# Working out the SSM poles on 128 partitions by 32 columns, from the first FFN steps on

## The chip, the cores and the metric

The kernel runs on one core of a Trainium2 chip. The metric is the device time of one execution in microseconds (us). A profiled execution gives, beside its time, a trace of every engine: TensorE (PE, with its weight loads as PEld), VectorE (DVE), ScalarE (ACT), GpSimd (POOL) and SyncE (SP, which issues most of the transfers). "SPq" is SP's queue of such issues.

## The reference

One layer of a hybrid encoder on 1024 tokens of width 1024, in float32:

```
x = x + 1/2 * SwiGLU_1(RMSNorm(x))              # 1024 -> 2816 -> 1024
[q | k | v | u] = RMSNorm(x) @ W_in
a = windowed attention (+-128 tokens, ALiBi, sinks) on (q, k, v)
s = bidirectional block-diagonal S5 SSM on u, GELU, GLU
x = x + concat(RMSNorm(a), RMSNorm(s)) @ W_out
x = x + 1/2 * SwiGLU_2(RMSNorm(x))
out = RMSNorm(x)
```

The SSM has 2 directions, 32 groups and 64 states to a group: 4096 complex poles. For each,

```
lr = min(lam_re, -1e-4); dt = exp(log_dt)        # one dt per direction and group
mag = exp(lr*dt)
a   = mag * (cos(li*dt) + i sin(li*dt))          # the pole
c   = (a - 1) / (lr + i li)                      # the coefficient
```

and from a and c come powers of the poles, decay tables and small matrices per group that the scan later reads.

## The kernel before

**The FFN.** Each matrix product is done in Strassen-Winograd form (class `Fast`), with seven products p in the order 1, 2, 6, 5, 7, 3, 4, and each float32 product is three matmuls of a high and a low part (`mm3`, L114 to L116). The work is a list of 217 units, one to a step: steps 0 to 139 make gate (i=0) and up (i=1) products, 14 to each of ten pairs s of hidden columns (pair 0 is done apart, in the startup, ahead of step 0); steps 140 to 216 are the down product, seven passes (p = 1, 2, 6, 5, 7, 3, 4) of eleven steps. A step is 12 matmuls of 512 columns.

`Fast.step(n)` issues, in this order: the loads of step n+6 (down product only, `load_down`, L267 and L274), the split of the operands of step n+3 (`prep`: ACT makes the high part, DVE the low part `ll`, with some Winograd sums on DVE), the 12 matmuls of step n, the evacuation of step n (`evac`: ACT or DVE reads the PSUM bank), and what is due at that step (`hidden`, `down_weights`: sums on DVE and stores through POOL). Products 1, 6, 7 and 4 of one (s, i) accumulate in the same PSUM bank, so step n+2 of them waits until the evacuation of step n has read the bank. Every engine works in the order of issue.

**The filler.** `ssm_tables()` is a generator. From step 17 on `fill(n)` runs one piece of it after a step: on 12 of every 14 steps of the gate and up products, then on all steps of the down passes p=1 and p=6 (twice on every second step of p=6). What is left after step 171 is run there. The generator has these pieces:

- step 17: loads of lam_re, lam_im, log_dt (L433 to L435) and of the skip gains;
- steps 18 to 35: the poles, a and c, on tiles of 32 partitions (groups) by 2 x 64 columns, 95 DVE instructions;
- step 40: four PE transposes (L540) into a PSUM bank, four ACT copies out of it;
- steps 41 to 51: powers and decay tables on 128 partitions (`cmul`, `p8r`, `ev`, `ec`, `bd`);
- steps 55 to 171: 32 groups g, three pieces each: `ca` (and `keep`, the stores of an earlier group's `vs` and `ks`), `vt` with a store, and `finish` (PE transposes and matmuls in the one "tp" bank, ACT copies to `vs` and `ks`). After every eight groups `spread` issues eight transfers from k_d to o_d in DRAM (L637): `spread(1)` at step 139, `spread(2)` at step 170, `spread(3)` at the end of step 171.

Pass p=2 of the down product also accumulates in "tp", which is why p=2 has no filler. During the passes p=1, 2, 6 and 5, four steps of each load a piece of x (L960).

**The startup** (ahead of step 0) loads eight row tiles of x, norms them (`prep_x`), turns them by PE transposes (`turn_tok`), forms Winograd sums on DVE (`sums_x`) and turns these (`turn_t`), and does pair 0 (`mm_first`, `evac_first`). Between steps 16 and 17 DVE builds `rel`, a table of distances; its first DVE instruction waits for a POOL iota behind POOL's stores.

Of the kernel before, what the change touches and what calls it, by code (L numbers as in the profile page):

```python
# [9 lines left out]
F32 = mybir.dt.float32  # L10
F32R = mybir.dt.float32r
I32 = mybir.dt.int32
BF16 = mybir.dt.bfloat16
AF = mybir.ActivationFunctionType
ALU = mybir.AluOpType
# [3 lines left out]
P = 128  # L19
# [11 lines left out]
G = 32  # L31
HC = 16
T = 8
# [34 lines left out]
def tile_hymba_block(  # L68
# [8 lines left out]
    V, S, PE, GP = nc.vector, nc.scalar, nc.tensor, nc.gpsimd  # L77
    load = nc.sync.dma_start
# [5 lines left out]
    pools = Pools(tc)  # L84


    def bank(tag, shape=(P, 512)):
        bufs = {"pg": 2, "pu": 2, "pd": 3, "tp": 1}[tag]
        return ps.tile(list(shape), F32, name=tag, tag=tag, bufs=bufs)

    def tt(out, a, b, op, eng=None):
        (eng or V).tensor_tensor(out=out, in0=a, in1=b, op=op)  # L92
# [46 lines left out]
    ident = const.tile([P, P], F32, name="ident")  # L139
# [277 lines left out]
    a64r = const.tile([P, G], F32, name="a64r")  # L417
    a64s = const.tile([P, 2, G], F32, name="a64s")

    def ssm_tables():  # L420
        tab = pools.open("tab")
        ev = tab.tile([P, 3, T, G], F32, name="ev")
        ec = tab.tile([P, 3, 11, G], F32, name="ec")
        dcol = tab.tile([48, G], F32, name="dcol")
        p1 = pools.open("p1")
        n1 = [0]

        def tl(shape=(32, 2, 64), dt=F32):
            n1[0] += 1
            return p1.tile(list(shape), dt, name=f"p1_{n1[0]}", tag=f"p1_{n1[0]}")  # L430

        lr, li, ldt = tl(), tl(), tl((32, 2))
        load(lr, lam_re[0].rearrange("d g p -> g d p"))  # L433
        load(li, lam_im[0].rearrange("d g p -> g d p"))
        load(ldt, log_dt[0].rearrange("d g -> g d"), )  # L435
        load(dcol[32:48], ssm_d[0].rearrange("g h -> h g"))
        yield
        e1, e2, e3 = tl(), tl(), tl()
        dt = tl((32, 2))

        def exp_(y, v, k, f, w):

            ts(v, v, -170.0, ALU.max, 88.8, ALU.min)
            ts(k, v, 1.4426950408889634, ALU.mult, MAGIC, ALU.add)
            ts(k, k, -MAGIC, ALU.add)
            stt(v, k, -0.693359375, v, ALU.mult, ALU.add)
            stt(v, k, 2.12194440e-4, v, ALU.mult, ALU.add)
            yield
            ts(y, v, 1.9875691500e-4, ALU.mult)
            for c in (1.3981999507e-3, 8.3334519073e-3, 4.1665795894e-2, 1.6666665459e-1,  # L450
                      5.0000001201e-1):
                stt(y, y, c, v, ALU.add, ALU.mult)
            yield
            tt(y, y, v, ALU.mult)
            tt(y, y, v, ALU.add)
            ts(y, y, 1.0, ALU.add)
            ts(f, k, 0.5, ALU.mult, MAGIC + 127.0, ALU.add)
            ts(w, f, -(MAGIC + 127.0), ALU.add)
            yield
            tt(k, k, w, ALU.subtract)  # L460
            ts(k, k, MAGIC + 127.0, ALU.add)
            ts(f.bitcast(I32), f.bitcast(I32), 23, ALU.logical_shift_left)
            ts(k.bitcast(I32), k.bitcast(I32), 23, ALU.logical_shift_left)
            tt(y, y, f, ALU.mult)
            tt(y, y, k, ALU.mult)

        yield from exp_(dt, ldt, e1[:, 0, 0:2], e2[:, 0, 0:2], e3[:, 0, 0:2])
        yield
        dtb = dt[:, :, None].to_broadcast([32, 2, 64])
        ts(lr, lr, -1e-4, ALU.min)  # L470
        arg, mag = tl(), tl()
        tt(arg, lr, dtb, ALU.mult)
        yield from exp_(mag, arg, e1, e2, e3)
        yield
        th, n, sn, cs, z = arg, tl(), tl(), tl(), tl()
        tt(th, li, dtb, ALU.mult)
        ts(n, th, 2.0 / math.pi, ALU.mult, MAGIC, ALU.add)
        b0 = tl(dt=I32)
        ts(b0, n.bitcast(I32), 1, ALU.bitwise_and)
        V.tensor_copy(e1, b0)  # L480
        ts(b0, n.bitcast(I32), 1, ALU.logical_shift_right, 1, ALU.bitwise_and)
# [18 lines left out]
        ts(cs, cs, 1.0, ALU.add)  # L500
        yield

        ar, ai = tl(), tl()
        ts(e3, e1, -1.0, ALU.mult, 1.0, ALU.add)
        tt(ai, sn, e3, ALU.mult)
        tt(z, cs, e1, ALU.mult)
# [14 lines left out]
        cr, ci, am = sn, cs, z  # L521
# [11 lines left out]
        tt(e2, am, li, ALU.mult)  # L533
        tt(ci, ci, e2, ALU.subtract)
        tt(ci, ci, e1, ALU.mult)
        for _ in range(5):
            yield
        tp = bank("tp", (P, 4, G))
        for j, src in enumerate((ar, ai, cr, ci)):
            PE.transpose(tp[:, j, :], src.rearrange("g d p -> g (d p)"), ident[:32, :32])  # L540
        cf = tab.tile([P, 2, G], F32, name="cf")
        cfs = tab.tile([P, 2, G], F32, name="cfs")
        pools.close("p1")
        p2 = pools.open("p2")
        pw = p2.tile([P, 2, 10, G], F32, name="pw")
        S.activation(pw[:, :, 1, :], tp[:, 0:2, :], AF.Copy)
# [107 lines left out]
        for gb in range(4):  # L654
# [8 lines left out]
            tp = bank("tp")  # L663
# [6 lines left out]
            for gi in range(8):  # L670
# [9 lines left out]
                g = 8 * gb + gi  # L680
# [30 lines left out]
    with tc.manual_schedule():  # L711
# [7 lines left out]
        f1 = Fast(ffn1_w_gate, ffn1_w_up, ffn1_w_down, "f1", first=1)  # L719
# [9 lines left out]
        tokp = pools.open("tok1")  # L729
# [12 lines left out]
        def load_x(*ts_):  # L742
            for t in ts_:
                load(tok[:, t, :], x_src[:, :, t, :])

        def load_first(i, f):

            for k in range(2):
                if f == 0:
                    f1.raw[0, i, k] = f1.ph.tile([P, 4, 256], F32, name="rawgu", tag=f"raw{i}{k}")  # L750
                load(f1.raw[0, i, k][:, :, f * P:(f + 1) * P],
                     f1.w[i][512 * k:512 * (k + 1), f * P:(f + 1) * P].rearrange("(k p) f -> p k f", p=P))
# [6 lines left out]
        load_x(2, 3)  # L759
        load_first(0, 1)  # L760
        load_first(1, 1)
        load_x(4, 5, 6, 7)

        def prep_x(t, how="pool", parts=1):
# [22 lines left out]
        def turn_tok(t):  # L787
            for n in range(2):
                turn_x(f"{n + 1}{t // 4 + 1}", tok[:, t, 512 * n:512 * (n + 1)], t % 4)

        def sums_x(q):
            r11, r21, r12, r22 = quarters(q)
            tt(r22, r22, r12, ALU.subtract)
            tt(r12, r12, r11, ALU.subtract)
            tt(r11, r22, r11, ALU.add)
            tt(r21, r21, r11, ALU.subtract)

        def turn_t(name, q):
            turn_x(name, quarters(q)[{"t2": 0, "t4": 1, "t1": 2, "t3": 3}[name]], q)
# [14 lines left out]
        def mm_first(i, f, h, c):  # L814
            if (i, f, h) not in accs:
                accs[i, f, h] = bank(("pg", "pu")[i])
            for d in range(2):
                hi, lo = lops[i, f, d]
                rh, rl = f1.X[f"{d + 1}{h + 1}"]
                for k in range(4):  # L820
                    mm3(accs[i, f, h][:, c], hi[:, k, :], lo[:, k, :], rh[:, k, c], rl[:, k, c],
                        d == 0 and k == 0, d == 1 and k == 3)

        def evac_first(f, h):
            st = tokp.tile([P, 512], F32, name="st", tag="st", bufs=2)
            S.activation(st, accs[0, f, h], AF.Silu)
            tt(f1.e0[0][{(0, 0): 0, (0, 1): 1, (1, 1): 2, (1, 0): 3}[f, h]], st, accs[1, f, h], ALU.mult)
# [31 lines left out]
        turn_tok(4)  # L859
        prep_x(6)  # L860
        mm_first(0, 1, 0, c01)
        turn_tok(5)
        prep_x(7)
        mm_first(1, 1, 0, c01)
        evac_first(1, 0)
        sums_x(0)
        mm_first(0, 0, 1, c0)
        turn_tok(6)
        mm_first(1, 0, 1, c0)
        sums_x(1)  # L870
        turn_tok(7)
        mm_first(0, 0, 1, c1)
        turn_t("t2", 0)
        turn_t("t2", 1)
        mm_first(1, 0, 1, c1)
        evac_first(0, 1)
        sums_x(2)
        f1.prep(0)
        turn_t("t1", 0)
        turn_t("t1", 1)  # L880
        mm_first(0, 1, 1, c01)
        sums_x(3)
        f1.prep(1)
        turn_t("t2", 2)
        turn_t("t1", 2)
        mm_first(1, 1, 1, c01)
# [8 lines left out]
        f1.hold(x1p.tile([P, NT * D], F32, name="evs", tag="x1"))  # L895
        for n in range(2, 17):
            f1.step(n)
            if n == 8:
                load(sink, attn_sinks.to_broadcast([P, HEADS]))
                for v_ in range(2):  # L900
                    load(aog[v_ * 64:(v_ + 1) * 64],
                         attn_out_norm[0, v_ * 256:(v_ + 1) * 256].rearrange("(m d) -> d m", d=64))
                load(sog, ssm_out_norm[0].rearrange("(k p) -> p k", p=P))
        pools.close("tok1")
        ts(nsink, sink, -1.0, ALU.mult)
        tab = pools.open("rel")
# [5 lines left out]
        tt(rel[:, 1], rel[:, 1], rel[:, 0], ALU.add)  # L912
        load(rel_d, rel[:, 1])
        pools.close("rel")
        tables = ssm_tables()

        def fill(n):
            if n >= f1.n1 or n % 14 > 1:
# [31 lines left out]
        for n in range(f1.n1, len(f1.units)):  # L950
            _, p, j = f1.units[n]
# [5 lines left out]
            if 3 <= j < 7 and p in (1, 2, 6, 5):  # L957
                h, c = {1: (0, 0), 2: (0, 1), 6: (1, 1), 5: (1, 0)}[p]
# [312 lines left out]
        for j in range(4):  # L1271
            for kv in range(2):
                h = 4 * kv + j
# [153 lines left out]
        for j in range(8):  # L1427
            acc = bank("pd", (P, 4, P))
            for i in range(4):
                g = 4 * j + i  # L1430
                o = om[g // 2]
# [88 lines left out]
        for t in range(NT + LAG):  # L1520
            if t < NT:
# [3 lines left out]
                z = bank("pu")  # L1525
# [47 lines left out]
        tokp = pools.open("tok2")  # L1573
# [74 lines left out]
        g = [tokp.tile([P, 4, P], F32R, name="g", tag=tag, bufs=2) for tag in ("sTh", "sTl") for _ in range(2)]  # L1648
        g = [a.rearrange("p k t -> p (k t)").bitcast(F32) for a in g]
# [62 lines left out]
        for n in range(f2.n1, len(f2.units) - TAIL):  # L1712
            _, p, j = f2.units[n]
# [63 lines left out]
```

## Time and profile before

| | before |
|---|---|
| time, median of 3 runs | 1793.89 us (1793.69 to 1797.38) |
| the profiled execution's own time | 1795.77 us |
| its span, first to last instruction | 1793.8 us |
| PE busy | 1723.0 us (96%) |
| DVE busy | 1249.5 us (70%) |
| ACT busy | 772.2 us (43%) |
| granted TensorE clock, mean | 0.984 |

The span is the stretch that the trace covers; about 2 us of the time lie outside it. PE is the engine that is nearly always at work, so time is gained or lost where PE waits.

### The profile page before, as it was taken

How to read it: one execution, taken by the hardware profiler on the slowest of the kernel's cores; microseconds unless marked ns; L12 is line 12 of the kernel's file. 1: busy time of each engine (PE TensorE's matmuls, PEld its weight loads, DVE VectorE, ACT ScalarE, POOL GpSimd, SP SyncE). 2: the span in 40 equal slices, each digit the busy share in tenths (PEclk: the TensorE clock that was granted, in tenths of full speed). 3: DMA queues.
4: the chain of work that ended last, by engine and by line, in shares of the span. 5: the costliest groups of instructions: out<-in, count | busy, mean ns of one | idle time of the engine just before them, and what ended most of it. 6: DMA issues, size and time to landing. Idle time of an engine off the chain costs nothing.

```text
span 1793.8 us, 23528 instructions
## 1 busy us (share of the span) xinstructions
PE 1723.0 (96%) x8120; PEld 1403.5 (78%) x8120; DVE 1249.5 (70%) x2230; ACT 772.2 (43%) x1462; POOL 272.8 (15%) x548
## 2 busy tenths in 40 slices
PE   8998999999999899999898999899999999999996
PEld 5887887777778688897666787788888888888884
DVE  5778998888877456557886466766766666755564
ACT  5333343333344345446586533443333333344444
POOL 1020100000000002215842003101111001100013
PEclk9999999999999999999889999999999999999998
DMA  6054545455588777411102513144545444586764
GB/s 160 29 206 143 197 147 169 160 166 172 171 268 249 192 250 231 156 60 40 48 1 70 206 59 116 38 170 156 167 146 181 160 147 161 180 289 221 222 189 141
DMA packets 178107, 279.57 MB, mean 156 GB/s; under 512 B 37570, under 2 KB 103362, under 8 KB 175172
## 3 DMA queue, kind: packets, MB, share of 16 engines
q1 hardware_dynamic: 160260, 208.34, 37.5%
q0 software_dynamic: 17728, 69.74, 11.0%
q8 instruction: 63, 1.03, 0.2%
q14 instruction: 56, 0.46, 0.1%
HBM read 192.92 MB, written 87.20 MB: 156 GB/s over the span
## 4 chain that ended last, share of the span: by engine, by line
PE 78%; DVE 9%; DMA 3%; ACT 3%; POOL 2%; issue 2%; SPq 2%; DVEq 0%; ACTq 0%; POOLq 0%
PE pd L114 10%; PE pd L115 10%; PE pd L116 10%; PE pu L114 7%; PE pu L116 7%; PE pu L115 7%; PE pg L114 7%; PE pg L115 6%; PE pg L116 6%; PE tp L616 1%; DVE s L92 1%; DVE sx L1296 1%; POOL b L92 1%; DVE evs L92 1%; PE tp L114 1%
## 5 line engine op out<-in xcount | busy, mean ns | idle before, releaser
L92 DVE TENSOR_TENSOR xb<-rawdown,xb 128x512 fp32r<-128x512 f32 x308 | 202.0, 697 | 134.5 <-ACT xb L106 132.1
L106 ACT ACTIVATE xb<-rawdown 128x512 fp32r<-128x512 f32 x308 | 179.8, 625 | 193.1 <-PE tp L115 74.5
L92 DVE TENSOR_TENSOR ll<-rawgu,lh 128x512 fp32r<-128x512 f32 x256 | 175.4, 687 | 118.4 <-ACT lh L106 117.9
L106 ACT ACTIVATE lh<-rawgu 128x512 fp32r<-128x512 f32 x256 | 159.6, 625 | 128.6 <-DVE rawgu L92 73.6
L92 DVE TENSOR_TENSOR evs<-evs 128x512 f32<-128x512 f32 x195 | 132.7, 688 | 3.9
L361 ACT ACTIVATE evs<-evs 128x512 f32<-128x512 f32 x49 | 31.0, 633 | 132.4 <-DVE evs L92 132.4
L114 PE MATMUL pd<-xb 128*128 128x512 f32 x198 | 78.0, 394 | 3.5 <-ACT xb L106 3.5
L115 PE MATMUL pd<-xb 128*128 128x512 f32 x198 | 78.0, 394 | 0.0
L116 PE MATMUL pd<-xb 128*128 128x512 f32 x198 | 77.8, 393 | 0.0
L115 PE MATMUL pg<-xb 128*128 128x512 f32 x176 | 69.1, 392 | 1.4 <-DVE xb L92 1.3
L114 PE MATMUL pg<-xb 128*128 128x512 f32 x176 | 70.0, 398 | 0.0
L116 PE MATMUL pg<-xb 128*128 128x512 f32 x176 | 68.5, 389 | 0.0
L116 PE MATMUL pu<-xb 128*128 128x512 f32 x176 | 68.5, 389 | 0.0
L114 PE MATMUL pu<-xb 128*128 128x512 f32 x176 | 68.5, 389 | 0.0
L115 PE MATMUL pu<-xb 128*128 128x512 f32 x176 | 68.5, 389 | 0.0
L114 PE MATMUL pd<-xb,lh 128*128 128x512 f32 x168 | 66.9, 398 | 0.0
L115 PE MATMUL pd<-xb,lh 128*128 128x512 f32 x168 | 65.9, 393 | 0.0
L116 PE MATMUL pd<-xb,ll 128*128 128x512 f32 x168 | 65.7, 391 | 0.0
L114 PE MATMUL pd<-xa,lh 128*128 128x512 f32 x160 | 62.8, 393 | 0.0
L115 PE MATMUL pd<-xa,lh 128*128 128x512 f32 x160 | 62.3, 389 | 0.0
L116 PE MATMUL pd<-xa,ll 128*128 128x512 f32 x160 | 62.3, 389 | 0.0
L378 POOL DMA_DIRECT2D f1h_d<-evs x73 | 39.0, 540 | 138.4 <-DVE ks L101 66.5
(546 smaller groups left out, 4814.6 us busy)
## 6 DMA issues: line engine op xcount, KB each, us to landing
evs<-in_ffn_w_down_dram SPq DMA_DIRECT2D x22, 1024.0 KB
rawgu<-in_ffn_w_gate_dram SPq DMA_DIRECT2D x42, 512.0 KB
rawgu<-in_ffn_w_up_dram SPq DMA_DIRECT2D x42, 512.0 KB
rawdown<-f1h_d SPq DMA_DIRECT2D x77, 256.0 KB
rawdown<-f2h_d SPq DMA_DIRECT2D x77, 256.0 KB
f1h_d<-evs POOLq DMA_DIRECT2D x73, 256.0 KB, 3.5
rawdown<-in_ffn_w_down_dram SPq DMA_DIRECT2D x66, 256.0 KB
f2h_d<-evs POOLq DMA_DIRECT2D x64, 256.0 KB, 3.0
```

The costliest lines, as they stand in the source:

```text
L92: (eng or V).tensor_tensor(out=out, in0=a, in1=b, op=op)
L106: S.activation(hi, src, AF.Copy)
L114: PE.matmul(acc, lhsT=lh, rhs=rh, start=first, stop=False, skip_group_check=more)
L115: PE.matmul(acc, lhsT=lh, rhs=rl, start=False, stop=False, skip_group_check=more)
L116: PE.matmul(acc, lhsT=ll, rhs=rh, start=False, stop=last, skip_group_check=more)
L361: S.activation(e, src, AF.Silu)
L378: store(self.h_d[s, p - 1], hs[p])
L616: PE.matmul(tp[:48, 256:432], lhsT=bd[:, c, :], rhs=ca[:, c].rearrange("p j h -> p (j h)"), start=c == 0, stop=c == 1)
L1296: V.tensor_tensor_reduce(out=q["sx"][kv][:, j, :nk], in0=sc, in1=bias[h][:, b0:b0 + nk], op0=ALU.add, op1=ALU.max, scale=1.0, scalar=-3e38 ...
```

## The change

The poles move out of `ssm_tables` into a generator of their own, `ssm_poles`, which works on thirteen tiles of 128 partitions (direction and state) by 32 columns (groups). Its inputs are loaded in the startup: lam_re and lam_im by rows into a tile that is free then (`f1.e0[0][3]`), log_dt by two loads that repeat it over 64 partitions each, all four ahead of the loads of x tiles 4 to 7. Two PE transposes turn lam_re and lam_im in the startup, into a "pd" bank, and DVE copies them out. Eight pieces of the generator are run in the startup, ten more after steps 2 to 11. Ahead of step 17 ACT copies the four results into the "tp" bank, from where the old copies take them. `ssm_tables` then starts with the powers, one piece ahead of step 17 and the next at step 17, so all later pieces come 22 to 24 calls earlier than before: `spread(1)` at step 115, `spread(2)` at step 141 and `spread(3)` at step 143. After step 143 there is no filler.

```diff
+    def ssm_poles(pool, raw):
+        tiles = [pool.tile([P, G], F32, name=f"pole{k}") for k in range(13)]
+        lr, li, e1, e2, e3, arg, mag, n, sn, cs, z, ldt, dt = tiles
+        for j, lam in enumerate((lam_re, lam_im)):
+            load(raw[:G, P * j:P * j + P].rearrange("g (d p) -> g d p", d=2), lam[0].rearrange("d g p -> g d p"))
+        for d in range(2):
+            load(ldt[64 * d:64 * d + 64], log_dt[0, d:d + 1, :].to_broadcast([64, G]))
+        yield
+        tp = bank("pd", (P, 4, P))
+        for j, o in enumerate((lr, li)):
+            PE.transpose(tp[:, j, :G], raw[:G, P * j:P * j + P], ident[:G, :G])
+            V.tensor_copy(o, tp[:, j, :G])
+        yield
...
-        for _ in range(5):
-            yield
-        tp = bank("tp", (P, 4, G))
-        for j, src in enumerate((ar, ai, cr, ci)):
-            PE.transpose(tp[:, j, :], src.rearrange("g d p -> g (d p)"), ident[:32, :32])
+        poles.extend((ar, ai, cr, ci))
...
         load_first(1, 1)
+        first = ssm_poles(tokp, f1.e0[0][3])
+        next(first)
         load_x(4, 5, 6, 7)
...
         mm_first(0, 1, 0, c01)
+        next(first)
         turn_tok(5)
...
         sums_x(0)
+        next(first)
...
         turn_tok(7)
+        next(first)
         mm_first(0, 0, 1, c1)
+        next(first)
...
         evac_first(0, 1)
+        next(first)
         sums_x(2)
         f1.prep(0)
+        next(first)
...
         f1.prep(1)
+        next(first)
...
             f1.step(n)
+            next(first, None)
...
+        tp = bank("tp", (P, 4, G))
+        for j, a in enumerate(poles):
+            S.activation(tp[:, j, :], a, AF.Copy)
...
-        tables = ssm_tables()
+        tables = ssm_tables(tp)
+        next(tables)
```

## Rows read from the trace of the kernel before

**Rows 1.** The page's first part: busy us (share of the span) xinstructions.

```profile
PE 1723.0 (96%) x8120; PEld 1403.5 (78%) x8120; DVE 1249.5 (70%) x2230; ACT 772.2 (43%) x1462; POOL 272.8 (15%) x548
```

**Rows 2.** Waits of PE from 130 to 300 us: total, times, longest.

```profile
PE pu L114 <- DVE evs L92: 2.9, 1, 2.9
PE pu L114 <- ACT evs L353: 1.1, 1, 1.1
PE pg L114 <- ACT evs L353: 0.6, 1, 0.6
```

**Rows 3.** Waits of PE from 600 to 650 us.

```profile
PE pd L114 <- ACT xb L106: 3.5, 1, 3.5
PE tp L114 <- ACT ks L621: 1.0, 1, 1.0
PE tp L614 <- ACT ks L621: 1.0, 1, 1.0
```

**Rows 4.** Timeline of PE: start, duration, in brackets the idle time before.

```profile
624.07 0.79 PE L114 MATMUL pd<-xb 128*128 128x512 f32 x1 [3.54 <-ACT xb L106]
...
629.65 0.42 PE L114 MATMUL pd<-xb 128*128 128x512 f32 x1
```

**Rows 5.** Windows: length; busy us (instructions) by engine; granted clock; DMA share; GB/s.

```profile
92.00:138.00 46.00, 46.00 (x205) 38.10 (x204) 35.28 (x59) 16.46 (x29) 9.31 (x17) 1.00 0.63 220
160.00:165.00 5.00, 2.08 (x9) 1.39 (x8) 4.83 (x15) 0.00 (x0) 0.00 (x0) 1.00 0.97 334
625.00:630.00 5.00, 5.00 (x13) 3.89 (x14) 3.25 (x5) 3.76 (x6) 0.00 (x0) 0.53 1.02 366
```

**Rows 6.** Groups by form, DVE, 138 to 200 us: busy us, mean ns.

```profile
L92 DVE TENSOR_TENSOR p<-p,p 32x128 f32<-32x128 f32 x30 | 7.7, 276 | 0.6
L526 DVE RECIPROCAL p<-p 32x128 f32<-32x128 f32 x1 | 0.9, 941 | 0.0
L92 DVE TENSOR_TENSOR p<-p,p 32x2 f32<-32x2 f32 x5 | 0.7, 145 | 0.1
```

**Rows 7.** Timeline of DVE in the startup and in steps 2 to 11.

```profile
55.60 0.69 DVE L92 TENSOR_TENSOR xa<-tp,xa 128x512 fp32r<-128x512 f32 x1 [0.40 <-ACT xa L106]
...
83.65 0.69 DVE L92 TENSOR_TENSOR xb<-pd,xb 128x512 fp32r<-128x512 f32 x1 [2.29 <-ACT xb L106]
...
95.29 0.69 DVE L92 TENSOR_TENSOR ll<-rawgu,lh 128x512 fp32r<-128x512 f32 x1 [1.65 <-ACT lh L106]
...
117.05 0.69 DVE L92 TENSOR_TENSOR ll<-rawgu,lh 128x512 fp32r<-128x512 f32 x1 [2.03 <-ACT lh L106]
...
118.62 0.69 DVE L92 TENSOR_TENSOR evs<-evs,pu 128x512 f32<-128x512 f32 x1 [0.28 <-PE pu L116]
```

**Rows 8.** Timeline of DVE from step 16 to step 19.

```profile
134.83 0.36 DVE L909 CAST rel<-rel 128x384 f32<-128x384 int32 x1 [2.06 <-POOL rel L908]
...
138.50 0.68 DVE L92 TENSOR_TENSOR evs<-evs,pg 128x512 f32<-128x512 f32 x1
143.47 0.35 DVE L98 TENSOR_SCALAR p<-p 32x2 f32<-32x2 f32 x2 [4.30 <-DMA p<-in_ssm_log_dt_dram]
```

**Rows 9.** Timeline of DVE, first and last row of the tables' pieces, steps 41 to 51.

```profile
208.55 0.09 DVE L562 MEMSET pw<- 128x32 f32 x1
...
238.22 0.79 DVE L606 MEMSET bd<- 128x384 f32 x2
```

**Rows 10.** Timeline of SP's queue: loads of x tiles and of lam_re.

```profile
22.09 6.84 SPq L744 DMA_DIRECT2D tok<-in_x_dram  x4
...
138.35 0.46 SPq L433 DMA_DIRECT2D p<-in_ssm_lambda_re_dram  x1
```

**Rows 11.** Timeline of SP's queue around the last two spreads.

```profile
600.07 5.10 SPq L637 DMA_DIRECT2D o_d<-k_d  x8
...
612.64 5.82 SPq L637 DMA_DIRECT2D o_d<-k_d  x8
618.51 0.59 SPq L267 DMA_DIRECT2D rawdown<-f1h_d  x1
```

More of the change, by code (lines that the diff above doesn't have):

```diff
@@ L418, in tile_hymba_block @@
     a64s = const.tile([P, 2, G], F32, name="a64s")
[L420 to L436, printed above, removed]
-        yield
-        e1, e2, e3 = tl(), tl(), tl()
-        dt = tl((32, 2))
+    def ssm_poles(pool, raw):
[5 more added lines that the diff above has]
+            load(ldt[64 * d:64 * d + 64], log_dt[0, d:d + 1, :].to_broadcast([64, G]))
+        yield
+        tp = bank("pd", (P, 4, P))
[3 more added lines that the diff above has]
+        yield
         def exp_(y, v, k, f, w):
@@ L465, in exp_ @@
             tt(y, y, k, ALU.mult)
-        yield from exp_(dt, ldt, e1[:, 0, 0:2], e2[:, 0, 0:2], e3[:, 0, 0:2])
+        yield from exp_(dt, ldt, e1, e2, e3)
         yield
-        dtb = dt[:, :, None].to_broadcast([32, 2, 64])
         ts(lr, lr, -1e-4, ALU.min)
-        arg, mag = tl(), tl()
-        tt(arg, lr, dtb, ALU.mult)
+        tt(arg, lr, dt, ALU.mult)
         yield from exp_(mag, arg, e1, e2, e3)
         yield
-        th, n, sn, cs, z = arg, tl(), tl(), tl(), tl()
-        tt(th, li, dtb, ALU.mult)
+        th = arg
+        tt(th, li, dt, ALU.mult)
         ts(n, th, 2.0 / math.pi, ALU.mult, MAGIC, ALU.add)
-        b0 = tl(dt=I32)
+        b0 = e3.bitcast(I32)
         ts(b0, n.bitcast(I32), 1, ALU.bitwise_and)
@@ L501, in ssm_tables @@
         yield
-        ar, ai = tl(), tl()
+        ar, ai = n, th
         ts(e3, e1, -1.0, ALU.mult, 1.0, ALU.add)
@@ L535, in ssm_tables @@
         tt(ci, ci, e1, ALU.mult)
-        for _ in range(5):
-            yield
-        tp = bank("tp", (P, 4, G))
-        for j, src in enumerate((ar, ai, cr, ci)):
-            PE.transpose(tp[:, j, :], src.rearrange("g d p -> g (d p)"), ident[:32, :32])
+        poles.extend((ar, ai, cr, ci))
+    poles = []
+    def ssm_tables(tp):
+        tab = pools.open("tab")
+        ev = tab.tile([P, 3, T, G], F32, name="ev")
+        ec = tab.tile([P, 3, 11, G], F32, name="ec")
+        dcol = tab.tile([48, G], F32, name="dcol")
         cf = tab.tile([P, 2, G], F32, name="cf")
         cfs = tab.tile([P, 2, G], F32, name="cfs")
-        pools.close("p1")
+        load(dcol[32:48], ssm_d[0].rearrange("g h -> h g"))
         p2 = pools.open("p2")
@@ L903, in tile_hymba_block @@
                 load(sog, ssm_out_norm[0].rearrange("(k p) -> p k", p=P))
+        for _ in first:
+            pass
+        tp = bank("tp", (P, 4, G))
+        for j, a in enumerate(poles):
+            S.activation(tp[:, j, :], a, AF.Copy)
         pools.close("tok1")
```

## Prediction

> **What bounds the kernel now.** First the page's busy line: PE is at work for 96% of the span [rows 1], so only what PE waits for, and its clock, can give time back. Second, PE's waits, window by window. Those that touch the moved code stand in two places. Between 130 and 300 us PE waits three times, 2.9, 1.1 and 0.6 us, each time for an evacuation that DVE or ACT made late [rows 2]. Between 600 and 650 us it waits 3.5 us for an operand and twice 1.0 us for the "tp" bank [rows 3]; and behind the 3.54 us come 12 matmuls that take 629.65 - 624.07 = 5.58 us [rows 4]. [...]
>
> Third, DVE's timeline, to see why. The waits of the first place start with DVE standing still 4.30 us for the load of log_dt, which was issued one step ahead of its first use [rows 8]; the 32-partition instructions of the poles then keep DVE from catching up. Fourth, SP's queue for the second place: `spread(2)` at 600.07 and `spread(3)` at 612.64 hold the queue until 618.51, when the load of step 178's operands goes out at last [rows 11]; PE restarts at 624.07 [rows 4].
>
> So before the change the moved code costs 4.6 us in steps 17 to 32 and 3.5 + 2.9 + 2.0 = 8.4 us at the end of pass p=6.
>
> **Price of one pole instruction.** On 32x128 a two-tensor instruction takes 276 ns, on 32x2 145 ns [rows 6]. No row has 128x32. Partitions work side by side, the columns count: 145 + 30 x (276-145)/126 = 176 ns, with the gap to the next I take 0.18 us (estimate). The bounds are the two rows themselves with their gaps, 0.153 and 0.258 us, these being the blocks of five to eight instructions in DVE's timeline divided by their count. The reciprocal is 941 ns at 128 columns; 0.36 us is my estimate for 32, 0.2 us more than the others.
>
> [...]
>
> **The startup.** Four small loads enter SP's queue ahead of x tiles 4 to 7. An issue of such a load takes 0.46 us [rows 10], so the tiles come up to 1.8 us later; the four tiles' own issues last 6.84 us because the queue is backed up [rows 10], so part of it is hidden. I take 0.3 us, bounds 0 and 1.8. Behind these issues wait `prep_x` on ACT and all that follows. The two transposes are two matmuls, at most 0.22 us each [rows 5]: 0.2 us on PE. DVE's two copies fall where it waits for POOL.
>
> On DVE the startup gets the dt part (22 instructions) and the first 13 for mag. The five right behind `sums_x(0)` are 0.9 us; DVE had 0.40 us to spare ahead of the next low part [rows 7], on which PE waits soon after: +0.5 us. Two blocks fall into idle time. The last three (19 instructions, 3.4 us) stand in a stretch where DVE is full, with 2.29 us to spare at its end [rows 7]: 1.1 us late for the low parts that free `turn_t`'s banks. Sum of the startup: 0.3 + 0.2 + 0.5 + 1.1 = +2.1 us; with 0.153 +1.2, with 0.258 and the loads at 1.8 +5.5.
>
> **Steps 2 to 32.** Steps 2 to 10 get 52 instructions, 9.4 + 0.2 = 9.6 us of DVE work, where it is busy 35.28 of 46 us [rows 5]. The idle pieces are six: 1.65 and 2.03 us, which take no more than the 0.9 and 1.1 us then to hand, 0.28, 1.85, 2.03 and 0.28 ([rows 7] show the first and the last two): 6.4 us. So step 11's evacuation, done at 119.31 before [rows 7], comes 3.2 us later. PE's step 13 adds into the same bank and starts 2.7 us after 118.6, when step 11 ended: it waits 1.2 us. DVE is then 2.0 us behind PE, and 3.4 with step 11's own eight instructions. There is no idle DVE time from there to `rel`, and the 2.06 us for POOL's iota [rows 8] move along, since the stores ahead of the iota wait for DVE. With the 0.65 us piece at step 17, step 18's evacuation is done at 139.2 [rows 8] + 1.2 + 3.4 + 0.65 = 144.4. PE's step 20 wants it eight steps after 118.6, at 140.2, + 1.2. It waits 3.0 us.
>
> From step 18 to 24 DVE had 4.3 us of waiting and 8.2 of poles (blocks of DVE's timeline), 12.5 us; with 140.2 - 139.2 = 1.0 us in hand at step 20 this cost PE 2.9 + 1.1 = 4.0 us [rows 2], so 7.5 us fit. Now it has the tables' pieces, which lie between 208.55 and 239 us before [rows 9]: 2.15, 0.65, 0.9, 2.15, 1.05, 1.45 and 1.85 = 10.2 us. With nothing in hand, PE waits 10.2 - 7.5 = 2.7 us, at step 27 as before. Steps 26 to 30 have no filler, so the 0.6 us goes. Sum: 1.2 + 3.0 + 2.7 - 4.6 = +2.3 us; +0.9 with 0.153, +6.5 with 0.258.
>
> Costed at nothing: the eight ACT copies ahead of step 17 (ACT is busy 16.46 of 46 us [rows 5]), the four transposes of step 40 that go, and steps 32 to 139, where the same pieces run 22 calls earlier under the same PE time.
>
> **The end of the tables.** All 8.4 us at the end of p=6 go, since p=6 has no filler now. What comes in its place: `spread(2)` at step 141 and `spread(3)` at 143, before the load of step 150. From the first spread's issue to PE's restart it took 624.07 - 600.07 = 24.0 us [rows 4, 11], and 3.5 us of that PE waited. Now there are eight steps (142 to 149) where there were seven, 2.7 us more cover, but one pair of loads more and one load of x stand in the queue, 1.5 us. If SP comes to `spread(2)` as late as before, PE waits 3.5 - 2.7 + 1.5 = 2.3 us. In p=1 loads of the first steps were issued early and SP may come to it some us sooner; then nothing. I take 1.0 us, bounds 0 and 6.4 (the old wait with the old clock). "tp" is not needed again before step 151, so its 2 us go.
>
> **Sum.** 2.1 + 2.3 - 8.4 + 1.0 = -3.0 us. On the profiled execution that is 1795.77 - 3.0 = 1792.8; it lies 1.9 us over the median of the runs shown, so for the median I say 1793.89 - 3.0 = 1790.9 us. A measurement of this kernel can't tell less than about 0.2%, 3.6 us, from no change.
>
> **Rivals.**
>
> A, the sum above (0.52): from -6.3 us (low price, no new wait) to about -1. Some three fifths of it lie beyond -3.6.
>
> B, DVE has room for the poles after all (0.14): the data waits that I counted as unusable take the blocks, and PE waits only at step 27 for the tables. Then -8.4 - (4.6 - 2.7) = -10.3 us, 1783.6. For it: DVE's idle share of steps 2 to 16 is 10.7 of 46 us [rows 5] for 11.0 us of blocks. Against it: from 118.6 on nothing of that is left.
>
> C, the two spreads stop PE at step 150 as they did at 178 (0.18): 2.1 + 2.3 - 8.4 + 6.4 = +2.4 us, 1796.3. For it: the same two spreads in the same order, now beside loads of x. Whether the clock falls decides 2.9 of the 6.4 us: it fell behind a wait of 3.54 us [rows 4, 5] and not in the window with the wait of 2.9 us [rows 2, 5]. [...]
>
> D, slower (0.16): DVE becomes the bound from the startup to step 20. If a 128x32 instruction costs what a 32x128 one does, 0.258 us, the startup costs 5.5 and steps 2 to 32 cost 6.5: 5.5 + 6.5 - 7.4 = +4.6 us, 1798.5. It decides from about 0.25 us with the loads fully exposed. For it: every instruction in the rows costs 145 ns at two columns. Against it: 276 against 145 ns says that columns count.
>
> **How the numbers follow.** Faster: three fifths of A (0.30) and B, 0.44. Same: the rest of A (0.22), two thirds of C (0.12) and a quarter of D (0.04), 0.38. Slower: a third of C, which has more queued behind it than before, and the rest of D, 0.18. The range 1784 to 1798 leaves out half of B and half of D, 0.15. For A alone it is 1787.5 to 1793.
>
> **What would show it.** Right: pole instructions of 0.15 to 0.2 us on 128x32; PE waits around 60 and 85 us some 2 us longer in all; new PE waits for `evs` near steps 13 and 20, one near 27; no wait for log_dt on DVE; no PE wait and no clock below 1.0 around 600 us; at step 150 at most a short wait for `xb`. Wrong: steps 2 to 20 without PE waits (B), a wait over 3 us with half the clock near 530 us (C), pole instructions near 0.25 us or x tiles 4 to 7 late by over 1 us (D).

## The result: slower

The changed kernel took 1804.26 us (median of five runs, 1800.9 to 1807.34) and the kernel before 1795.73 us beside it (five runs): ratio 1.0053, 95% interval 1.0033 to 1.0073, so 5.9 to 13.1 us slower. The forecast was 1790.9 us and its range ended at 1798. The profiled execution of the changed kernel took 1800.9 us, the least of the five, with a span of 1798.7 us. Two executions further down, one of r4 (2450.88 us) and one of r9 (1932.88 us), are slow ones and are left out of the ratios.

The busy line of its page answers to [rows 1]. PE's work is the same within 1.2 us; of the 4.9 us by which the span grew, 3.7 are time in which PE stands.

```profile
PE 1724.2 (96%) x8118; PEld 1405.3 (78%) x8118; DVE 1247.7 (69%) x2232; ACT 772.9 (43%) x1466; POOL 273.4 (15%) x548
```

**The startup.** These are waits of PE in the changed kernel from 0 to 130 us (total, times, longest). The one with L431 and the one of `tp` for `tok` are not in the kernel before, and the one for `xb` was 0.2 us there.

```profile
PE pd L777 <- DVE tok L101: 4.5, 2, 3.5
PE pd L431 <- DVE pole L432: 3.3, 1, 3.3
...
PE pd L777 <- DVE xb L92: 1.3, 1, 1.3
...
PE tp L777 <- DVE tok L101: 1.0, 1, 1.0
```

L431 issues the two transposes of the poles' inputs, and L432 the copy of each. The timeline of PE, and then that of DVE, at the same place:

```profile
47.08 0.24 PE L431 MATMUL pd<-ident,u 32*128 32x32 f32 x1
50.59 0.31 PE L431 MATMUL pd<-ident,u 32*128 32x32 f32 x1 [3.27 <-DVE pole L432]
50.84 1.97 PE L777 MATMUL pd<-ident,tok 128*128 128x128 f32 x8
```

```profile
47.80 0.68 DVE L92 TENSOR_TENSOR xa<-pd,xa 128x512 fp32r<-128x512 f32 x1
49.15 1.28 DVE L101 SCALAR_TENSOR_TENSOR tok<-tok,rq,gb 128x1024 f32<-128x1024 f32 x1 [0.68 <-POOL rq L92]
50.35 0.18 DVE L432 COPY pole<-pd 128x32 f32<-128x32 f32 x1
50.94 0.19 DVE L432 COPY pole<-pd 128x32 f32<-128x32 f32 x1 [0.41 <-PE pd L431]
```

The first transpose is done at 47.3 us. Its copy stands in DVE's order behind the subtraction at 47.80 us and the scaling of x tile 6, which itself waits 0.68 us for POOL; it runs at 50.35 us. The second transpose writes the same tile of PSUM and goes only then, after 3.27 us, and with it everything on PE behind it. PE is busy for 2.33 us of the 5 us from 45 us on, and in the next window the clock falls (windows of PE: length, busy us, granted clock, DMA share, GB/s):

```profile
45.00:50.00 5.00, 2.33 (x11) 1.00 0.79 265
50.00:55.00 5.00, 4.41 (x17) 0.66 0.26 92
```

The second thing is the queue of SP; these rows answer to [rows 10].

```profile
22.38 5.08 SPq L425 DMA_DIRECT2D u<-in_ssm_lambda_re_dram  x1
...
27.97 1.17 SPq L427 DMA_DIRECT2D pole<-in_ssm_log_dt_dram  x2
29.18 2.55 SPq L740 DMA_DIRECT2D tok<-in_x_dram  x4
```

The four tiles are all issued at 29.18 + 2.55 = 31.73 us, 9.35 us after the first issue shown. Before, with nothing ahead of them, that took 6.84 us, so they go out 2.5 us later. PE's wait of 1.0 us in `tp` for `tok` is for one of them.

**Steps 2 to 32.** PE's timeline, only the rows in which it waits for an evacuation; they answer to [rows 2].

```profile
130.93 0.50 PE L114 MATMUL pu<-xa,lh 128*128 128x512 f32 x1 [0.78 <-DVE evs L92]
...
145.35 0.50 PE L114 MATMUL pg<-xa,lh 128*128 128x512 f32 x1 [0.51 <-ACT evs L353]
...
152.76 0.50 PE L114 MATMUL pg<-xa,lh 128*128 128x512 f32 x1 [1.67 <-DVE evs L92]
...
175.36 0.50 PE L114 MATMUL pu<-xa,lh 128*128 128x512 f32 x1 [3.25 <-DVE evs L92]
```

These are steps 13, 18, 20 and 27, and the sum is 6.2 us where 4.6 us stood before. The clock was 0.69 from 175 to 180 us, behind the last of them.

**The end of the tables.** At the end of pass p=6 one wait of 0.6 us is left of [rows 3] (waits of PE from 560 to 760 us), and a new one stands at step 150 (500 to 560 us):

```profile
PE pd L115 <- DVE xb L92: 0.6, 1, 0.6
```

```profile
PE pg L114 <- ACT xb L106: 2.4, 1, 2.4
```

The window of PE behind it:

```profile
555.00:560.00 5.00, 4.76 (x13) 0.66 1.05 275
```

The queue of SP ahead of it has the two spreads, as in [rows 11], now with stores and loads of x between them and the operands:

```profile
526.72 5.27 SPq L633 DMA_DIRECT2D o_d<-k_d  x8
...
542.64 5.04 SPq L633 DMA_DIRECT2D o_d<-k_d  x8
547.99 0.66 SPq L972 DMA_DIRECT2D x<-in_x_dram  x1
548.76 0.39 SPq L267 DMA_DIRECT2D rawdown<-f1h_d  x1
```

### The profile page after: what moved, and what is told of

The parts are those of the page before. It is cut to its first block, busy times and chain, and to the rows that moved or that the text cites. A ratio compares the mean times of both kernels' runs of the same rounds, so it can differ in the third digit from the quotient of the medians.

```text
span 1798.7 us, 23524 instructions
## 1 busy us (share of the span) xinstructions
PE 1724.2 (96%) x8118; PEld 1405.3 (78%) x8118; DVE 1247.7 (69%) x2232; ACT 772.9 (43%) x1466; POOL 273.4 (15%) x548
## 4 chain that ended last, share of the span: by engine, by line
PE 77%; DVE 10%; issue 4%; ACT 3%; POOL 3%; DMA 2%; SPq 1%; DVEq 0%; ACTq 0%; POOLq 0%
PE pd L114 10%; PE pd L115 10%; PE pd L116 10%; PE pu L114 7%; PE pu L115 7%; PE pu L116 7%; PE pg L114 6%; PE pg L115 6%; PE pg L116 6%; PE tp L612 1%; POOL b L92 1%; DVE s L92 1%; DVE sx L1308 1%; PE tp L114 1%; PE tp L116 1%
```

## How the traces were laid side by side

Executions differ in their first 30 us, before anything of the change: the first matmul on x tiles 2 and 3 (`pg<-xr`, behind a wait for ACT) began at 32.31 us in the first profile of the kernel before and at 29.61 us in a second one. From that matmul on, the startups of kernels with the same code there agree to 0.02 us (before, b2, r5), 0.20 (r4, r7) and 0.24 (r3, r6, r8). Each is one trace, so a difference of less than some 0.3 us says nothing. So two stretches are taken from each trace: from that matmul to step 2's evacuation by ACT (the startup), and from there to the last block of DVE's subtractions for FFN1's down operands (`xb<-rawdown,xb`, four in a row, step 216). These are the three starts and the two differences, in us:

```
kernel                     matmul   evacuation   block    startup   rest of FFN1
before                      32.31      94.14     726.33    61.83      632.19
b2 (before, again)          29.61      91.46     724.72    61.85      633.26
after                       32.93     102.99     734.14    70.06      631.15
r1 turns first              30.87      97.92     727.12    67.05      629.20
r2 loads behind             31.97      98.53     728.44    66.56      629.91
r3 both                     29.40      93.42     725.14    64.02      631.72
r4 layout, late             30.89      92.93     718.07    62.04      625.14
r5 before, early spreads    32.44      94.27     723.93    61.83      629.66
r6 r3, early spreads        31.54      95.32     724.10    63.78      628.78
r7 r4, early spreads        31.48      93.32     716.60    61.84      623.28
r8 r6, tables from 25       29.98      94.00     715.76    64.02      621.76
r9 r7, early inputs         32.52     103.26     727.37    70.74      624.11
```

The changed kernel loses 8.2 us in the startup and wins 1.0 us in the rest of FFN1 against the first profile of before, 2.1 us against the second.

The theory that the runs were to test: the startup's loss is the second transpose, held up behind DVE's order, and the place of the four loads. The rival is that of the prediction, D: DVE's own work on the poles fills the startup.

## The experiments

Each kernel was run in turn with the kernel before (6 to 12 runs of each kernel, 23 to 30 of before). r1 to r4 ran in one session, on one chip; b2 and r5 to r7 in a second one and r8 and r9 in a third, on another chip. So kernels of different sessions are compared only by what each is over or under before.

**r1, both transposes ahead of both copies.** PE no longer waits between them.

```diff
-            PE.transpose(tp[:, j, :G], raw[:G, P * j:P * j + P], ident[:G, :G])
-            V.tensor_copy(o, tp[:, j, :G])
+        for j in range(2):
+            PE.transpose(tp[:, j, :G], raw[:G, P * j:P * j + P], ident[:G, :G])
+        for j, o in enumerate((lr, li)):
+            V.tensor_copy(o, tp[:, j, :G])
```

> One edit to the changed kernel: both transposes of the poles' inputs are issued ahead of both copies, so the second no longer waits for the copy of the first. Theory S (the loss is made in the startup, by the 3.3 us wait of TensorE for that copy and the half clock behind it, and by late x tiles): the wait goes, the clock stays at 1.00 around 50 us, step 2's evacuation comes some 4.5 us earlier than in the changed kernel, and the time is about 1804.3 - 4.5 = 1800. Rival D (VectorE is overloaded by the pole instructions, wherever TensorE shows it first): the wait moves to the next place, and the time stays within 1.5 us of the changed kernel's. Rival C (the two spreads): nothing moves either.

**r2, the four small loads behind those of x tiles 4 to 7.**

```diff
+        load_x(4, 5, 6, 7)
         first = ssm_poles(tokp, f1.e0[0][3])
         next(first)
-        load_x(4, 5, 6, 7)
```

> One edit to the changed kernel: the four small loads are issued behind the loads of x tiles 4 to 7 and not ahead of them. Theory S: tiles 4 and 5 are at hand 2.2 and 3.6 us earlier, TensorE's 1.0 us wait at 40 us goes, VectorE comes to the copy earlier, so the 3.3 us wait shrinks to about 1 us with no low clock behind it; the time is about 1804.3 - 4.5 = 1800. Rival D: within 1.5 us of the changed kernel's. If the four loads cost nothing on SP's queue, as a range of 0 to 1.8 us had it, at most 1.8 us come back.

**r3, both edits.**

> Both edits at once. Theory S: of the 8.9 us by which step 2 is late, the wait (3.3), the clock (about 1.5) and the late tiles (1.0) go; 2 to 3 us stay, which is what was forecast for VectorE's blocks in the startup. Time about 1804.3 - 6 = 1798.3, still 2 to 3 us over the kernel before, because steps 2 to 27 (+1.6 us and a low clock near 172 us) and the wait at step 150 (2.4 us) stay. Rival D: 1803 or more.

Measured: r1 1795.85 us, ratio 1.0019 (1.0006 to 1.0032); r2 1795.59 us, 1.0012 (0.9999 to 1.0026); r3 1795.43 us, 1.0024 (1.0007 to 1.0041); before 1792.19 us. Each edit alone gives back some 5 us of the 8.5, as expected, and r3 stands 3.2 us over before, where 2 to 3 were expected. By the times r3 is no better than either, and the three intervals overlap. The traces are sharper: the startup is 67.05 us in r1, 66.56 in r2, 64.02 in r3, against 70.06 in the changed kernel, so the order of the transposes is worth 3.0 us alone, the place of the loads 3.5 us, and the two together 6.0 us. PE's timeline in r1:

```profile
45.58 0.30 PE L431 MATMUL pd<-ident,u 32*128 32x32 f32 x2
...
47.73 0.66 PE L778 MATMUL pd<-ident,tok 128*128 128x128 f32 x4 [1.25 <-DVE xa L92]
```

The pair takes 0.30 us now, near the 0.2 that the prediction gave it; the wait of 1.25 us behind it is not in r3, where the tiles' loads go first. In r2 the loads of the tiles are issued as before the change, and the second transpose still waits:

```profile
47.68 0.24 PE L431 MATMUL pd<-ident,u 32*128 32x32 f32 x1 [1.89 <-DVE pole L432]
```

```profile
21.83 6.66 SPq L740 DMA_DIRECT2D tok<-in_x_dram  x4
28.53 0.46 SPq L425 DMA_DIRECT2D u<-in_ssm_lambda_re_dram  x1
...
29.50 1.17 SPq L427 DMA_DIRECT2D pole<-in_ssm_log_dt_dram  x2
```

In r3 2.2 us of the startup's loss are left (64.02 - 61.83). Two waits of PE for DVE show most of it. These are their rows in PE's timeline of the kernel before, and then of r3:

```profile
60.32 0.38 PE L115 MATMUL pg<-xa,lh 128*128 128x256 f32 x1 [0.58 <-DVE xa L92]
...
84.39 0.66 PE L779 MATMUL pd<-ident,tok 128*128 128x128 f32 x4 [0.15 <-DVE xb L92]
```

```profile
58.51 0.38 PE L115 MATMUL pg<-xa,lh 128*128 128x256 f32 x1 [1.05 <-DVE xa L92]
...
83.68 0.66 PE L778 MATMUL pd<-ident,tok 128*128 128x128 f32 x4 [1.25 <-DVE xb L92]
```

They are 0.47 and 1.10 us longer. The prediction gave the pole arithmetic 0.5 + 1.1 = 1.6 us, and these are the places that it named: the low part behind `sums_x(0)`, and the low parts that free `turn_t`'s banks. In r9 below, which has no pole instruction in the startup, both waits are as before (0.6 and 0.2 us). The pair of transposes is another 0.3 us, and the last 0.3 us stay open.

**r4, the layout alone.** The poles are worked out on 128x32 with inputs turned by PE, but loaded at step 17 and turned three pieces later; nothing is left in the startup and in steps 2 to 16, and the tables follow where they were.

```diff
-        first = ssm_poles(tokp, f1.e0[0][3])
-        next(first)
...
+        p1 = pools.open("p1")
+        yield from ssm_poles(p1, p1.tile([P, 2 * P], F32, name="raw"))
+        yield
```

> The layout alone: 128 partitions by 32 columns, inputs turned by TensorE, but loaded at step 17 as before, turned three pieces later, and worked out from step 22 on; nothing in the startup or in steps 2 to 16, and the tables end where they ended before. Theory S with the forecast's price: no wait for log_dt on VectorE, pole pieces of 1.0 to 1.4 us where they were 1.4 to 2.1, so TensorE's 4.6 us of waits between 140 and 180 us fall to under 1.5 us, while the 8.4 us at the end of pass p=6 stay; about 1795.7 - 3.5 = 1792. Rival (narrow tiles of fixed cost per instruction save nothing): within 1.5 us of the kernel before.

Measured: 1783.82 us, ratio 0.9954 (0.9938 to 0.997), faster by 8.4 us, more than expected. The waits of [rows 2] are gone altogether (4.6 us), and at the end of p=6 2.2 and 0.4 us for `xb` are left where 5.5 us stood; against that the waits for `tp` from 300 to 500 us have grown from 1.7 to 4.4 us. So in the new layout, worked out late, the poles are a gain, and what lost was the place to which the work was moved. Two things make the gain, and no run separates them: DVE's pole instructions take 16.5 us in all where they took 21.2, and since three pieces pass between the loads and their first use, DVE's 4.30 us of standing still for log_dt [rows 8] is gone. The kernel before with nothing but earlier loads was not run.

**b2, the kernel before again**, for a second profile.

> The kernel before, unchanged, for a second profile of it. If the 8.4 us at the end of the tables are a fixed cost, this profile shows them again: one PE wait of 3 to 4 us between 600 and 650 us, a window with the clock near half behind it, and two waits of 1.0 us. If the half clock belonged to the one execution that was profiled, the wait is there and the clock stays at 1.00, so only some 5.5 us were there to be won. The ratio of the times is 1.000 within 0.0015 in either case.

Measured: 1794.54 us, ratio 1.0002 (0.9991 to 1.0013). The waits of PE from 560 to 760 us, and a window of PE behind the first of them:

```profile
PE pd L114 <- ACT xb L106: 2.9, 1, 2.9
PE tp L614 <- ACT ks L621: 1.1, 1, 1.1
PE tp L114 <- ACT ks L621: 1.1, 1, 1.1
PE tp L614 <- DVE x L101: 1.0, 1, 1.0
```

```profile
625.00:630.00 5.00, 5.00 (x16) 0.65 1.04 350
```

The loss at the end of the tables is no accident of one execution: wait, fallen clock and both `tp` waits come again.

**r5, the kernel before with early spreads.** The spread of a group of eight is issued in the middle of the next group, not at its end; only `spread(3)` is left at the end.

```diff
                 if gi == 4 and gb < 3:
                     nxt = load_bc(gb + 1)
+                if gi == 4 and gb:
+                    spread(gb - 1)
...
-            if gb:
-                spread(gb - 1)
```

> The kernel before with one edit: spread(0), spread(1) and spread(2) are issued in the middle of the next group of eight and not at its end, so that only spread(3) stands at the end of the tables. If the two spreads in a row stop PE at step 178, this alone gives back 5.5 to 8.4 us: 1784 to 1787 us, and no PE wait over 1 us between 600 and 650 us. If the loads of step 178 were late for another reason, the wait stays and the time is within 2 us of before.

Measured: 1790.63 us, ratio 0.9979 (0.9966 to 0.9992), 3.0 us faster; expected were 5.5 to 8.4. The wait for `xb` is gone, so the spreads were its cause, but in its place PE waits for a bank (560 to 760 us):

```profile
PE tp L614 <- ACT ks L621: 3.8, 1, 3.8
```

PE waits there for the bank until ACT has copied `vs` and `ks` out of it, and ACT's timeline shows what ACT itself waits for:

```profile
603.90 0.38 ACT L619 ACTIVATE vs<-tp 128x256 f32<-128x256 f32 x1 [5.23 <-DMA v_d<-vs]
```

The buffer comes free only when an earlier store of `vs` has landed. Why that store lands late was not tested. The clock falls here too, to 0.66 from 605 to 610 us. So 5.4 of the 8.4 us came back, as another wait and another stretch at a low clock, some 20 us earlier in the kernel.

**r6, r3 with early spreads.**

> r3_both (both transposes ahead of both copies, small loads behind those of tiles 4 to 7) with the same early spreads. r3_both stood 3.2 us over before and its PE waited 2.6 us for xb at step 150, with the clock at 0.97 of full between 500 and 560 us (1.8 us). If the two spreads caused that, both go: 1791 us, 1 us under before, and no wait for xb between 500 and 560 us. If the wait there is for loads of x or for the load queue as such, the time stays at 1795 us.

Measured: 1792.35 us, ratio 0.9991 (0.9979 to 1.0002). The median moved as expected, from 3.2 us over before to 1.3 us under it, but PE still waits 1.62 us at step 150 behind `spread(3)` alone (PE's timeline), and in the traces the rest of FFN1 is only 0.4 to 2.9 us shorter than in r1, r2 and r3. How much of the 4.5 us is the spreads' stays open.

```profile
544.75 0.49 PE L114 MATMUL pg<-xb 128*128 128x512 f32 x1 [1.62 <-ACT xb L106]
```

**r7, r4 with early spreads.**

> r4_layout_late (128x32 layout, everything from step 17, nothing in the startup) with the same early spreads. r4_layout_late measured 8.4 us under before and PE still waited 2.2 us for xb at the end of its tables. If the spreads cause that wait, it goes: 1781.5 us, ratio 0.994. If it is the load queue as such, 1783.8 us as r4_layout_late.

Measured: 1782.29 us, ratio 0.9938 (0.9926 to 0.9949), 11.3 us faster than before. This is the fastest of all kernels here. Of the waits for operands at the end of p=6 0.2 us are left.

**r8, r6 with the tables called from step 25.** The poles stay early; the tables' pieces no longer follow them without a pause.

```diff
         for n in range(17, f1.n1):
-            f1.step(n, fill)
+            f1.step(n, fill if n >= 25 else None)
```

> r6_both_early_spread with the pieces of the tables called from step 25 on, not from step 17; the poles stay in the startup and in steps 2 to 12. r6_both_early_spread measured 1.3 us under before; its PE waited 0.8, 0.5 and 1.6 us at steps 13, 18 and 20, and 3.2 us at step 27. If the first three belong to the poles and the fourth to the tables' pieces that follow them without a pause, the first three stay (2.9 us in all) and the fourth goes: 4.5 us under before, 1789 us. If a DVE that is late since step 12 makes all four, the fourth stays or moves eight steps on, and the time stays at 1 to 2 us under before.

Measured: 1785.24 us, ratio 0.9959 (0.9943 to 0.9974), 8.0 us under before (1793.26) by the medians, where 4.5 were expected. The wait of 3.2 us at step 27 is gone, so it belonged to the tables' pieces behind the poles. Waits of PE from 130 to 300 us:

```profile
PE pg L114 <- DVE evs L92: 1.0, 1, 1.0
PE tp L662 <- ACT ks L618: 0.7, 1, 0.7
PE pg L114 <- ACT evs L353: 0.5, 1, 0.5
```

The wait for `xb` at step 150 has gone too (for `tp` 1.2 and 0.7 us stand between 500 and 560 us), which the expectation had not asked for.

**r9, r7 with the changed kernel's early inputs alone.** Four loads ahead of those of tiles 4 to 7, and the two transposes, each with its copy behind it; the results are not used and no pole is worked out early.

> r7_late_early_spread (everything from step 17, 11.3 us under before) plus one thing of the change alone: four small loads ahead of those of x tiles 4 to 7 and the two transposes with a copy behind each, as in the changed kernel; their results are not used, and no pole is worked out there. In the traces the loads' place was worth 3.5 us (r1 against r3) and the order of the transposes 3.0 us (r2 against r3). If these two are all of the startup's surprise, step 2's evacuation comes 6 to 6.5 us later, counted from the first matmul on x tiles 2 and 3, and the time rises by the same: 1788.5 us, 5 us under before. If DVE's work on the poles in the startup has a part in it, it rises by less than 3 us.

Measured: 1789.7 us, ratio 0.998 (0.9964 to 0.9996). Against r7's ratio that is 0.42%, 7.5 us. In the trace the startup is 8.9 us longer than r7's (70.74 - 61.84); the profiled execution took 1797.71 us, 8.0 over the median, but 4.5 us of what it is over r7's lie in the rest of the program, behind FFN1. PE's timeline and windows show the same picture as in the changed kernel, with a longer wait and a lower clock:

```profile
51.46 0.31 PE L430 MATMUL pd<-ident,u 32*128 32x32 f32 x1 [4.08 <-DVE pole L431]
```

```profile
50.00:55.00 5.00, 3.54 (x13) 0.52 0.74 254
55.00:60.00 5.00, 5.00 (x19) 0.80 0.05 17
```

So a loss as large as the changed kernel's comes without one pole instruction in the startup, and the rival D falls: of the 8.2 us it has no more than the 2.2 that r3 shows. The size was not as expected, 7.5 us for 6 to 6.5: the parts do not simply add. PE's wait was longer here, 4.08 us for 3.27, and the clock fell lower, to 0.52 where the changed kernel had 0.66.

## Why the prediction was wrong, point by point

**The startup is the step that failed**: +2.1 us forecast, 8.2 measured. Its terms one by one:

- The two transposes, "0.2 us on PE", cost 3.0 us (r3 against r2 and r1 against the changed kernel bound it by 2.5 and 3.0). The cost of the matmuls themselves was right, 0.30 us for the pair in r1. What failed is the sentence behind it, that DVE's two copies "fall where it waits for POOL". DVE does wait there, but the copy stands behind that wait and behind the scaling of 1.28 us that does the waiting, and PE waits with it, because the second transpose writes the tile that the first copy reads. The prediction looked for what the copies cost DVE, not for who waits for them: it had named no wait that the change adds there.
- The loads, "0.3 us, bounds 0 and 1.8", cost 3.5 us (r1 against r3: 3.0). The bound was four issues of 0.46 us [rows 10], and the argument was that part of them is hidden, since the queue is full. In r2, behind the tiles, the four take 30.67 - 28.53 = 2.14 us; ahead of them they put the last tile off by 2.5 us. So nothing of them was hidden: the tiles' own issues became shorter, 2.55 us for 6.84, only because the first small load stood 5.08 us in their place. The startup lost 0.5 to 1.0 us more than the tiles' 2.5; where is not shown. Late tiles ("late by over 1 us") were to be a sign of D; the sign came without D.
- The arithmetic on DVE, "0.5 + 1.1 = 1.6 us", was right: the two waits in r3 are 0.47 and 1.10 us longer. The 2.2 us that are left in r3 hold the pair of transposes as well.
- The low bound, "with 0.153 +1.2", takes the loads at nothing, which the prediction does not say; with 0.3 us for them it is 1.5.
- The startup's half clock had no term at all: 0.66 between 50 and 55 us, and 0.50 in it from 51 to 54 us, behind a window in which PE was busy for 2.33 of 5 us. It is contained in the prices above.

**The price of a pole instruction was right.** The prediction had put 0.18 us between the rows of [rows 6]. These groups of DVE from 60 to 130 us (busy us, mean ns) show what it was:

```profile
L92 DVE TENSOR_TENSOR pole<-pole,pole 128x32 f32<-128x32 f32 x27 | 4.7, 190 | 0.5
...
L96 DVE TENSOR_SCALAR pole<-pole 128x32 f32<-128x32 f32 x16 | 2.8, 178 | 0.3
...
L518 DVE RECIPROCAL pole<-pole 128x32 f32<-128x32 f32 x1 | 0.4, 353 | 0.0
```

The two-tensor instructions took 190 ns where the prediction drew 176 between the rows. That partitions work side by side, as it had it, the trace of the kernel before shows in the tables' instructions (DVE by form): 128x32 takes 189 ns there, and 128x128 takes 288 where 32x128 takes 276 [rows 6], 4% more for four times the partitions.

```profile
L92 DVE TENSOR_TENSOR pw<-w,w 128x32 f32<-128x32 f32 x4 | 0.6, 189 | 0.1
...
L92 DVE TENSOR_TENSOR pw<-w,w 128x128 f32<-128x128 f32 x2 | 0.5, 288 | 0.0
```

**Steps 2 to 32 were right in mechanism and near in size.** Forecast were waits of 1.2 us at step 13, 3.0 at step 20 and 2.7 at step 27, +2.3 us in all. Measured were 0.8 at step 13, 0.5 and 1.7 at steps 18 and 20, 3.2 at step 27, +1.6 us. r8 confirms the last: with a pause ahead of the tables it is gone. Not forecast was the fallen clock behind it, which was worth 1.7 us (below).

**The end of the tables: the term for the new wait was too small.** The 8.4 us at the end of p=6 went, all but 0.6, as forecast. The 2.9 us for the clock in them are the 5.58 us of the twelve matmuls [rows 4] less 12 x 46.0/205 = 2.7 us [rows 5]; the granted clock was 0.53 there, and 0.65 in b2. The wait at step 150, "I take 1.0 us, bounds 0 and 6.4", measured 2.4 us, and with it 0.2 and 0.6 us of other waits for `xb`; the clock fell behind it to 0.66 between 555 and 560 us. It is C's mechanism in a smaller size, beside A's sum. r5 shows too that the old 8.4 us were not to be had by moving the spreads alone: there a wait of 3.8 us for `tp` came up in their place. In the changed kernel no piece of the tables is left in p=6 that could wait for it.

**The sum.** The rest of FFN1 was forecast at 2.3 - 8.4 + 1.0 = -5.1 us; measured are -1.0 and -2.1 against the two profiles of before, a miss of 3.0 to 4.1. In it are the waits for `xb` (2.4 + 0.2 + 0.6 - 1.0 = 2.2 us) and the clock at step 27 (1.7), less 0.7 for the smaller evacuation waits: 3.2 us. The fallen clock behind step 150 was not priced by a run. Reckoned as the prediction does it, the twelve matmuls from 555.02 to 559.96 us, less 0.22 us of waiting among them, took 4.7 us for 2.7, so some 2.0 us (estimate). Together that is 5.2 us, more than the miss, so between 1.1 and 2.2 us came out better than forecast elsewhere; where stays open. With the startup, 8.2 - 1.0 = +7.2 us for the trace, 8.2 - 2.1 = +6.1 against the second profile; the medians say +8.5 (interval 5.9 to 13.1). The rest of the program, which the change does not touch, is 1063.3 to 1068.1 us in the twelve profiles (span less block), 1064.6 in the changed kernel's, so executions differ there by up to 4.8 us, and the traces show no part of the loss in it.

## What to carry to other kernels

Before a small operation is put into an engine that sets the pace, ask who it waits for and what stands ahead of that work in the other engine's order; two transposes into one tile with a copy between them tied PE to DVE's order here, for 3.27 us, and both transposes first, then both copies, cost 0.3 us. A full queue hid nothing of the small loads put ahead of large ones: here the large ones went out 2.5 us later, all of the small ones' issue time (2.14 us in r2), and 0.5 to 1.0 us more was lost behind them. A change that both cheapens work and moves it should be tried as two: here the new layout, with its loads ahead of their use, was worth 8.4 us, 11.3 with early spreads, and the move ate more than all of it.

## What the runs showed of the hardware that was not expected

The same wait of PE, in the same code, lowered the clock in one execution and not in another. At step 27 PE waited 3.20 to 3.25 us in the changed kernel and in r1, r2, r3 and r6; the granted clock was 1.00 behind it in r1, r2 and r6, and fell in the changed kernel and in r3 (each is one execution). The window of r3 that holds the matmul behind the wait, and that of r6:

```profile
165.00:170.00 5.00, 4.26 (x12) 0.67 0.86 187
```

```profile
165.00:170.00 5.00, 2.36 (x10) 1.00 1.07 249
```

The mean of 0.67 has a lower clock in part of the window: in r3 the matmuls of step 27 start 0.42 to 0.43 us apart from 166.79 to 169.78 us, and 0.23 us apart from 170.18 us on; in the changed kernel, in windows of 1 us, the clock was 0.50 from 177 to 180 us. From step 2's evacuation to one that lies behind step 27 r3 and the changed kernel took 87.87 and 87.93 us, and r1, r2 and r6 took 86.25 us each: the lower clock cost 1.6 to 1.7 us where it came. The wait of 3.2 us was thus worth its own time or half as much again, and one trace shows only one of the two.

The kernel before shows the same with one and the same code. Its wait of 2.92 us at step 27, on which the prediction rested that the clock stays up behind such a wait (rival C), ends at 163.73 us in the first profile and at 161.04 us in the second, b2. The window behind it in the first, and in b2:

```profile
165.00:170.00 5.00, 5.00 (x23) 1.00 0.03 9
```

```profile
160.00:165.00 5.00, 3.96 (x11) 0.66 0.48 138
```

In b2 the step behind the wait took 1.5 us longer, but a later wait of PE for an evacuation (0.6 us, [rows 2]) was gone, and by step 35 only 0.3 us of it were left. So the lower clock cost its full time only where no later wait of PE took it up.
